# Another order of work in the first stage of a fused encoder block on one Trainium2 core

## The chip, the core and the metric

The kernel runs on one core of a Trainium2 chip. The metric is the device time of one execution in microseconds (us); lower is better. Engines are named as in the profile: PE (TensorE, the matrix products), DVE (VectorE), ACT (ScalarE), POOL (GpSimd) and SP (SyncE, which issues nearly all DMAs here).

## What is computed

One layer of a post-norm block on 256 tokens of width 1024, all in float32. Cut to what matters here:

```python
mod = silu(c) @ w_ada + b_ada                  # (1, 6144)
sh1, sc1, g1, sh2, sc2, g2 = split(mod, 6)
u = normalize(x) * (1 + sc1) + sh1             # (256, 1024)
proj = u @ w_in                                # q, k, v of 8 heads, a forget gate, gated linear attention, merge gates
x = post_norm(alpha * x + (1 + g1) * mixer(proj), ln1_g, ln1_b)
u = normalize(x) * (1 + sc2) + sh2
x = post_norm(alpha * x + (1 + g2) * moe(u), ln2_g, ln2_b)   # top 4 of 32 experts
```

The mixer is a forgetting attention of 8 heads, a gated linear attention of 4 heads, their two output projections, a gated merge and one more projection. The experts read 403 MB of weights, most of all that is loaded.

## The kernel before, in words

The program has three parts. The **first stage** (lines 587 to 849) makes u and the q, k and v of the attention. The **dense blocks** multiply u and what follows from it by the rest of w_in, the branch weights and w_out; side tasks (attention, gates, scans) are put between their products by a planner, `Tasks` with `Pace`, which keeps an estimated clock for each engine and lets a task take its next step when that clock says that its inputs are there. The **expert stage** streams the weights of 32 experts. All loads go through `Ring`, which issues the next load on SP's queue as soon as a buffer is free, in the fixed order in which the loads were asked for. A list of 12 buffers is open to it in the first stage, so that its loads run several rounds ahead.

Everything in the first stage is written out by hand, in program order, and each engine works through its instructions in that order. For accuracy a dense operand is split in two: `split` (line 674) has ACT write the high part in the fast float32 format (fp32r) and DVE or POOL the difference to the original; `three` (line 451) then issues three products, high by high, high by low, low by high.

The stage runs over k = 0 to 7, 128 input features each. What belongs to a k:

- `ada_sum(k)` (line 762): 16 products of 32 x 256 of `csrep`, the silu of c laid out over 32 columns, with a block of w_ada of 1 MB (two DMAs). They leave four partial sums of shift and scale in the PSUM bank `pa`.
- `ada_cols(k)` (line 773): DVE copies the sums to SBUF (`mod`, in the buffer LQ); two products of one column each ("the columns" below) add the four parts up and turn them to a column in the bank `pb`; DVE adds the bias (`shc`); ACT writes the high part of u (`uh`, buffer U1), DVE u itself in place (`nT`, buffers GS and GX) and then the low part (`ul`, buffer U2).
- `row_parts(k)` (line 785): ACT, DVE and POOL split the rows of w_in for q and k (1024 columns, the low part in two halves, one on DVE and one on POOL) and for v (512 columns, low part on POOL), into two of the buffers W0, W1, AD, AM.
- 24 products of 256 columns for q and k, 6 products of 512 columns for v.
- two steps of `masks()` (line 640), a generator that builds the mask constants on DVE: 13 instructions up to the first `yield`, then 3 for each of six levels.

Ahead of them x is normalised (lines 617 to 628) and transposed by PE, in four groups of four transposes, `x_T(hf, tb)` (line 750): `hf` is the half of the features, `tb` the half of the tokens. PE's order in the loop of before is (lines 809 to 829):

```python
sums[k + 1] = ada_sum(k + 1)
for cb in range(8): three(...)            # q and k products of k
ahead[k + 1] = row_parts(k + 1)
ada_cols(k + 1, sums.pop(k + 1))
for tb in range(2): three(pv[tb], ...)    # v products of k
next(ms, None); next(ms, None)            # two steps of the masks
```

After k = 7's q and k products stand 24 products of 32 columns for the forget and low-rank gates (`ff_mm`, line 731), and the dense blocks follow.

All engine calls go through a wrapper, so that the profile gives line 209 for every instruction; they are told apart by tiles. A tile's name in the profile is that of its buffer: a pair such as W0 and W1 stands as W, U1 and U2 as U1U, GS and GX as GSGX; `b` is a PSUM bank.

Of the kernel before, what the change touches and what calls it, by code (L numbers as in the profile page):

```python
# [377 lines left out]
def block_kernel(ctx, tc, x, c, w_ada, b_ada, w_in, fox_f_bias, w_gla_gate, b_gla_gate, gla_norm_g,  # L378
# [236 lines left out]
        ACT.activation(mv[:, 2:3], mv[:, 3:4], AF.Exp, scale=-0.5)  # L615

    nT = gst.now([128, 4, T]), gst.now([128, 4, T])
    for tb in range(2):
        st = bn_tile()
        for i in range(2):  # L620
            DVE.bn_stats(st[:, i, :], xn[tb][:, i * 512:(i + 1) * 512])
        mv = mean_var(st)
        rstd(mv)
        if tb:
            DVE.tensor_scalar(xn[tb], xn[tb], mv[:, 0:1], mv[:, 2:3], op0=OP.subtract, op1=OP.mult)
        else:
            DVE.scalar_tensor_tensor(mv[:, 3:4], mv[:, 0:1], -1.0, mv[:, 2:3], op0=OP.mult, op1=OP.mult)
            ACT.activation(xn[tb], xn[tb], AF.Identity, bias=mv[:, 3:4], scale=mv[:, 2:3])


    strict = small("strict", [128, 128], BF16)
# [8 lines left out]
    def masks():  # L640
        trio = consts.now([128, 128])
        DVE.tensor_scalar(trio, jp, 0.0, None, op0=OP.is_ge)
        DVE.tensor_scalar(strict, jp, 0.0, None, op0=OP.is_gt)
        DVE.tensor_scalar(after, jp, 0.0, NEG, op0=OP.is_gt, op1=OP.mult)
        DVE.tensor_copy(identb, ident)
        DVE.memset(onesb, 1.0)
        DVE.tensor_copy(trior[:, 0:128], trio)
        DVE.tensor_copy(trior[:, 128:256], ones)
        xr = consts.now([128, 128], I32)
        DVE.tensor_tensor(xr, pi, ji, op=OP.bitwise_xor)  # L650
        xrf = consts.now([128, 128])
        DVE.tensor_copy(xrf, xr)
        DVE.tensor_scalar(tri64, xrf, 64.0, 1.0 / 16.0, op0=OP.is_lt, op1=OP.mult)
        DVE.tensor_tensor(tri64, tri64, trio, op=OP.mult)
        upm = consts.now([128, 128])
        DVE.scalar_tensor_tensor(upm, jp, 0.0, xrf, op0=OP.is_gt, op1=OP.mult)
        a = consts.now([128, 64])
        yield
        for L in LEVELS:
            yield  # L660
            m = lvl[L] = small(f"lv{L}", [128, 64])
            u3 = upm.rearrange("p (n two l) -> p n two l", two=2, l=L)[:, :, 1, :]
            DVE.tensor_scalar(m.rearrange("p (n l) -> p n l", l=L), u3, float(L), None, op0=OP.is_ge)
            DVE.tensor_scalar(a.rearrange("p (n l) -> p n l", l=L), u3, float(2 * L), None, op0=OP.is_lt)
            DVE.tensor_tensor(m, m, a, op=OP.mult)
# [96 lines left out]
    def ada_sum(c):  # L762

        w = ring[first["a", c]].rearrange("p k a n -> p k (a n)")
        s = pa[:, c % 2 * 256:c % 2 * 256 + 256]
        for k in range(KC):
            j = k % 4
            PE.matmul(s[32 * j:32 * j + 32, :], csrep[:, k, :], w[:, k, :],
                      start=(k < 4), stop=(k >= 4), skip_group_check=True)
        done(first["a", c])  # L770
        return s

    def ada_cols(c, s):
        mod = la.now([128, 256])
        DVE.tensor_copy(mod, s)
        for i in range(2):
            PE.matmul(pb[:, 2 * c + i:2 * c + i + 1], mod[:, i * 128:(i + 1) * 128], stack[:, 0:1], start=True, stop=True)
        la.put(mod)
        DVE.tensor_tensor(shc[:, :, c], pb[:, 2 * c:2 * c + 2], cols[:, 16 + c:32:8], op=OP.add)
        u = nT[c // 4][:, c % 4, :]  # L780
        ACT.activation(uh[:, c, :], u, AF.Identity, bias=shc[:, 0, c:c + 1], scale=shc[:, 1, c:c + 1])
        DVE.tensor_scalar(u, u, shc[:, 1, c:c + 1], shc[:, 0, c:c + 1], op0=OP.mult, op1=OP.add)
        DVE.tensor_tensor(ul[:, c, :], u, uh[:, c, :], op=OP.subtract)

    def row_parts(k):
        w = ring[first["w", k]]
        qk = split(w[:, 0:2, :].rearrange(FLAT), DVE if k else POOL, POOL)
        v = split(w[:, 2, :], POOL)
        done(first["w", k])
        return qk, v  # L790

    def back():
        for n in ("AD", "AM"):
            if reg[n] in pair.free:
                pair.free.remove(reg[n])

    LA = 2
    ms = masks()
    for tb in range(2):
        x_T(0, tb)  # L800
    pa, pb = aux.now(), aux.now()
    sums = {0: ada_sum(0)}
    ahead = {0: row_parts(0)}
    ada_cols(0, sums.pop(0))
    for tb in range(2):
        x_T(1, tb)
    gle.put(*xn)
    pqk, pv = [mm.now() for _ in range(4)], [aux.now(), aux.now()]
    for k in range(KC):
        qk, v = ahead.pop(k)  # L810
        if k + 1 < KC:
            sums[k + 1] = ada_sum(k + 1)
        for cb in range(8):
            cs = slice(cb * 128, (cb + 1) * 128)
            three(pqk[cb // 2][:, (cb % 2) * T:(cb % 2 + 1) * T], (qk[0][:, cs], qk[1][:, cs]), u_of(k),
                  k == 0 and cb % 2 == 0, k == KC - 1)
        pair.put(qk[2])
        if k + 1 < KC:
            ahead[k + 1] = row_parts(k + 1)
            ada_cols(k + 1, sums.pop(k + 1))  # L820
        if k == KC - 1:
            back()
            for q in range(LA):
# [1292 lines left out]
```

## Time and profile before

| | |
|---|---|
| median of 3 runs | 1268.77 us (1267.07 to 1268.92) |
| the profiled execution | 1269.44 us, span 1267.6 us |
| mean granted TensorE clock | 0.988 |
| PE busy | 1170.3 us, 92% of the span |
| DVE, ACT, POOL busy | 494.6, 265.5, 73.2 us |
| loaded | 471.57 MB, 372 GB/s over the span |

Times in the rows further down are us from the start of the span. A row of the timeline gives start, duration, engine, line, operation, out<-in, shapes and the number of instructions merged into it; in brackets the idle time of the engine just before it and what ended that. SPq is SP's queue of DMA issues. Busy times overlap across engines, and PE's ends are modelled, so starts say more than ends.

### The profile page before, as it was taken

The page shows a single profiled execution, that of the slowest core. Times are in us where ns is not written, and L with a number is a line of the kernel's source. Part 1 is how long each engine was busy: PE and PEld are TensorE (multiplying, and loading weights), DVE is VectorE, ACT ScalarE, POOL GpSimd, SP SyncE. Part 2 cuts the span into 40 slices and gives each one's busy share as a digit, 9 for nine tenths or more (in the row PEclk, how much of TensorE's full clock was granted, in tenths as well). Part 3 has the DMA queues.
Part 4 walks back from the last instruction along what each step waited for, and adds up shares of the span by engine and source line. Part 5 has one row for each costly group of instructions (what it writes and reads, how often), then busy time and mean ns, then how long its engine had stood idle before and what let it go on. Part 6 is the DMA issues. An engine that isn't in the chain of part 4 may idle for free. (4 is left out here: it accounts for less than half of the span.)

```text
span 1267.6 us, 15762 instructions
## 1 busy us (share of the span) xinstructions
PE 1170.3 (92%) x6482; PEld 601.1 (47%) x6482; DVE 494.6 (39%) x1070; ACT 265.5 (21%) x525; POOL 73.2 (6%) x53
## 2 busy tenths in 40 slices
PE   6999999999699999999989989898989898889995
PEld 4797777898434434344333424242433333343432
DVE  5646754477433232324322232222233232222333
ACT  3355445443311111011010101010101101010101
POOL 3412322010000000000000000000000000000000
PEclk9999999999799899999999999999999999999998
DMA  9954347995999999999999999999999999999994
GB/s 306 317 160 133 133 164 263 392 355 226 373 400 429 413 427 428 428 426 428 428 428 429 426 427 429 425 429 428 427 426 429 429 425 428 428 428 428 427 413 143
DMA packets 74118, 471.57 MB, mean 372 GB/s; under 512 B 8637, under 2 KB 29149, under 8 KB 47034
## 3 DMA queue, kind: packets, MB, share of 16 engines
q1 hardware_dynamic: 73850, 470.23, 91.2%
q8 instruction: 53, 0.87, 0.3%
q10 hardware_dynamic: 192, 0.27, 0.1%
q14 instruction: 23, 0.19, 0.0%
HBM read 469.44 MB, written 1.05 MB: 371 GB/s over the span
## 5 line engine op out<-in xcount | busy, mean ns | idle before, releaser
L209 PE MATMUL b<-U1U,W 128*128 128x256 f32 (+1 forms) x840 | 143.1, 410 | 10.8 <-DMA U1U<-in_w_down_dram 8.3
L209 DVE COPY W<-b 128x512 f32<-128x512 f32 x32 | 22.1, 692 | 291.7 <-PE b L209 291.7
L209 PEld LDWEIGHTS b<-U1U,W 128*128 128x128 f32 (+1 forms) x840 | 86.8, 170 | 69.6 <-issue 60.4
L209 DVE TENSOR_TENSOR W<-b,SP 128x512 f32<-128x512 f32 (+1 forms) x33 | 22.3, 676 | 221.3 <-PE b L209 221.3
L209 DVE TENSOR_TENSOR GL<-b,GL 128x512 f32<-128x512 f32 x124 | 77.0, 684 | 54.0 <-PE b L209 54.0
L209 PE MATMUL b<-YB1NB,W 128*64 128x512 f32 (+2 forms) x440 | 89.4, 528 | 5.7 <-DVE SP L209 4.0
L209 PE MATMUL b<-YAW,W 128*64 128x512 f32 (+1 forms) x384 | 82.3, 555 | 6.5 <-DVE SP L209 5.3
L209 PE MATMUL b<-R2YB,W 128*64 128x512 f32 x344 | 78.2, 595 | 8.9 <-DMA R2YB<-in_w_down_dram 7.1
L209 PE MATMUL b<-GSGX,W 128*64 128x512 f32 x336 | 76.2, 595 | 10.3 <-DMA GSGX<-in_w_down_dram 8.5
L209 PE MATMUL b<-R0R,W 128*64 128x512 f32 (+1 forms) x368 | 80.2, 578 | 4.1 <-DMA R0R<-in_w_up_dram 3.7
L209 PE MATMUL b<-LQFA,W 128*64 128x512 f32 x336 | 78.5, 610 | 3.9 <-DMA LQFA<-in_w_up_dram 3.9
L209 ACT ACTIVATE W<-b 128x512 f32<-128x512 f32 x32 | 19.1, 597 | 298.7 <-PE b L209 298.7
L209 PE MATMUL b<-GVKB,W 128*64 128x512 f32 x336 | 76.4, 597 | 5.0 <-DMA GVKB<-in_w_up_dram 5.0
L209 PE MATMUL b<-ADAM,W 128*64 128x512 f32 x336 | 75.9, 593 | 4.0 <-DVE SP L209 4.0
L209 ACT ACTIVATE SP<-b 128x256 f32<-128x256 f32 (+1 forms) x34 | 12.8, 377 | 308.7 <-PE b L209 308.7
L209 PEld LDWEIGHTS b<-W,QA 128*128 128x128 f32 x512 | 63.6, 202 | 15.1 <-DVE GL L209 11.4
L209 PE MATMUL b<-W,QA 128*128 128x128 f32 x512 | 66.7, 291 | 0.5 <-DVE rk L209 0.5
L209 PE MATMUL b<-W,SP 64*128 64x512 f32 (+1 forms) x264 | 63.9, 602 | 0.5 <-DVE W L209 0.5
L209 PEld LDWEIGHTS b<-YB1NB,W 128*64 128x64 f32 (+1 forms) x440 | 35.7, 146 | 56.4 <-issue 45.0
L209 ACT ACTIVATE W<-b,scol 128x128 f32<-128x128 f32 x124 | 46.8, 456 | 65.7 <-PE b L209 60.0
L209 POOL TENSOR_TENSOR GL<-GL,QB 128x512 f32<-128x512 f32 x2 | 2.9, 1426 | 954.1 <-ACT GL L209 954.0
L209 PEld LDWEIGHTS b<-YAW,W 128*64 128x64 f32 (+1 forms) x384 | 30.7, 144 | 55.0 <-issue 43.3
(339 smaller groups left out, 1383.5 us busy)
## 6 DMA issues: line engine op xcount, KB each, us to landing
GVKB<-in_w_up_dram SPq DMA_DIRECT2D x21, 2048.0 KB
R0R<-in_w_up_dram SPq DMA_DIRECT2D x20, 2048.0 KB
LQFA<-in_w_up_dram SPq DMA_DIRECT2D x20, 2048.0 KB
YB1NB<-in_w_up_dram SPq DMA_DIRECT2D x11, 2048.0 KB
U1U<-in_w_up_dram SPq DMA_DIRECT2D x11, 2048.0 KB
YAW<-in_w_up_dram SPq DMA_DIRECT2D x11, 2048.0 KB
GSGX<-in_w_up_dram SPq DMA_DIRECT2D x11, 2048.0 KB
YAW<-in_w_down_dram SPq DMA_DIRECT2D x10, 2048.0 KB
```

The lines of the kernel that those rows point to most:

```text
L209: r = f(*a, **k)
```

## The change

- x: both halves of the tokens are normalised by DVE; before, ACT did the first.
- `ada_sum(0)` comes ahead of all transposes. Of the transposes, x_T(1, 0) comes behind the columns of k = 0, x_T(1, 1) and `ada_sum(1)` between the two halves of the q and k products of k = 0.
- The copy of the sums to SBUF belongs to `ada_sum` now, right behind its products.
- In each round the columns and all of `ada_cols(k + 1)`, then the split of the weights of k + 1, stand between the first and the second half of the q and k products of k (for k = 0 behind both). In the loop of before the split stood ahead of `ada_cols`.
- For k = 0 the split is written out: the first half of the low part goes to DVE instead of POOL, behind the low part of u.
- `masks()` gets more `yield`s: two or three DVE instructions for a step.

```diff
     nT = gst.now([128, 4, T]), gst.now([128, 4, T])
+    mvs = []
     for tb in range(2):
         st = bn_tile()
         for i in range(2):
             DVE.bn_stats(st[:, i, :], xn[tb][:, i * 512:(i + 1) * 512])
-        mv = mean_var(st)
-        rstd(mv)
-        if tb:
-            DVE.tensor_scalar(xn[tb], xn[tb], mv[:, 0:1], mv[:, 2:3], op0=OP.subtract, op1=OP.mult)
-        else:
-            DVE.scalar_tensor_tensor(mv[:, 3:4], mv[:, 0:1], -1.0, mv[:, 2:3], op0=OP.mult, op1=OP.mult)
-            ACT.activation(xn[tb], xn[tb], AF.Identity, bias=mv[:, 3:4], scale=mv[:, 2:3])
+        mvs.append(mean_var(st))
+        rstd(mvs[tb])
+    for tb, mv in enumerate(mvs):
+        DVE.tensor_scalar(xn[tb], xn[tb], mv[:, 0:1], mv[:, 2:3], op0=OP.subtract, op1=OP.mult)
...
         DVE.tensor_scalar(strict, jp, 0.0, None, op0=OP.is_gt)
+        yield
         DVE.tensor_scalar(after, jp, 0.0, NEG, op0=OP.is_gt, op1=OP.mult)
         DVE.tensor_copy(identb, ident)
+        yield
         DVE.memset(onesb, 1.0)
         DVE.tensor_copy(trior[:, 0:128], trio)
         DVE.tensor_copy(trior[:, 128:256], ones)
+        yield
         xr = consts.now([128, 128], I32)
         DVE.tensor_tensor(xr, pi, ji, op=OP.bitwise_xor)
         xrf = consts.now([128, 128])
         DVE.tensor_copy(xrf, xr)
+        yield
         DVE.tensor_scalar(tri64, xrf, 64.0, 1.0 / 16.0, op0=OP.is_lt, op1=OP.mult)
         DVE.tensor_tensor(tri64, tri64, trio, op=OP.mult)
+        yield
         upm = consts.now([128, 128])
         DVE.scalar_tensor_tensor(upm, jp, 0.0, xrf, op0=OP.is_gt, op1=OP.mult)
         a = consts.now([128, 64])
-        yield
         for L in LEVELS:
             yield
...
         done(first["a", c])
-        return s
-
-    def ada_cols(c, s):
         mod = la.now([128, 256])
         DVE.tensor_copy(mod, s)
+        return mod
+
+    def ada_cols(c, mod):
...
-    def row_parts(k):
-        w = ring[first["w", k]]
-        qk = split(w[:, 0:2, :].rearrange(FLAT), DVE if k else POOL, POOL)
-        v = split(w[:, 2, :], POOL)
+    def qk_parts(k):
+        return split(ring[first["w", k]][:, 0:2, :].rearrange(FLAT), DVE, POOL)
+
+    def v_parts(k):
+        v = split(ring[first["w", k]][:, 2, :], POOL)
         done(first["w", k])
-        return qk, v
+        return v
...
+    def qk_mm(k, qk, cbs):
+        for cb in cbs:
             cs = slice(cb * 128, (cb + 1) * 128)
             three(pqk[cb // 2][:, (cb % 2) * T:(cb % 2 + 1) * T], (qk[0][:, cs], qk[1][:, cs]), u_of(k),
                   k == 0 and cb % 2 == 0, k == KC - 1)
...
-    for tb in range(2):
-        x_T(0, tb)
     pa, pb = aux.now(), aux.now()
-    sums = {0: ada_sum(0)}
-    ahead = {0: row_parts(0)}
-    ada_cols(0, sums.pop(0))
+    mods = {0: ada_sum(0)}
     for tb in range(2):
-        x_T(1, tb)
-    gle.put(*xn)
-    pqk, pv = [mm.now() for _ in range(4)], [aux.now(), aux.now()]
+        x_T(0, tb)
+    ahead = {}
+    part_0 = ring[first["w", 0]][:, 0:2, :].rearrange(FLAT)
+    t0 = pair.now()
+    wh0, wl0 = t0[:, 0:1024].bitcast(F32R), t0[:, 1024:2048].bitcast(F32R)
+    ACT.activation(wh0, part_0, AF.Copy)
+    POOL.tensor_tensor(wl0[:, 512:1024], part_0[:, 512:1024], wh0[:, 512:1024], op=OP.subtract)
+    ada_cols(0, mods.pop(0))
+    DVE.tensor_tensor(wl0[:, 0:512], part_0[:, 0:512], wh0[:, 0:512], op=OP.subtract)
+    ahead[0] = (wh0, wl0, t0), v_parts(0)
+    x_T(1, 0)
+    pqk = [mm.now() for _ in range(4)]
     for k in range(KC):
         qk, v = ahead.pop(k)
-        if k + 1 < KC:
-            sums[k + 1] = ada_sum(k + 1)
-        for cb in range(8):
-            cs = slice(cb * 128, (cb + 1) * 128)
-            three(pqk[cb // 2][:, (cb % 2) * T:(cb % 2 + 1) * T], (qk[0][:, cs], qk[1][:, cs]), u_of(k),
-                  k == 0 and cb % 2 == 0, k == KC - 1)
+        if 0 < k < KC - 1:
+            mods[k + 1] = ada_sum(k + 1)
+        qk_mm(k, qk, range(4))
+        if k == 0:
+            mods[1] = ada_sum(1)
+            x_T(1, 1)
+            gle.put(*xn)
+            pv = [aux.now(), aux.now()]
+            qk_mm(k, qk, range(4, 8))
+        if k + 1 < KC:
+            ada_cols(k + 1, mods.pop(k + 1))
+            ahead[k + 1] = qk_parts(k + 1), v_parts(k + 1)
+        if k:
+            qk_mm(k, qk, range(4, 8))
         pair.put(qk[2])
-        if k + 1 < KC:
-            ahead[k + 1] = row_parts(k + 1)
-            ada_cols(k + 1, sums.pop(k + 1))
```

PE at the start of the stage, from behind the transposition of the small vectors to the first columns of k = 1. Products of `ident` are transposes of x (buffer GL), 32x256 are the sums of w_ada, 128x1 the columns, 128x256 the q and k products (a row is one bank, 6 products). Before:

```order
L209 MATMUL b_68<-ident,GL 128x128 x4
L209 MATMUL b_69<-ident,GL 128x128 x4
L209 MATMUL b_70<-YB1NB,LQFA 32x256 x8
L209 MATMUL b_67<-stack,LQFA 128x1 x2
L209 MATMUL b_68<-ident,GL 128x128 x4
L209 MATMUL b_69<-ident,GL 128x128 x4
L209 MATMUL b_70<-QB,LQFA 32x256 x8
L209 MATMUL b_63<-U1U_71,W_72 128x256 x6
L209 MATMUL b_64<-U1U_71,W_72 128x256 x6
L209 MATMUL b_65<-U1U_71,W_72 128x256 x6
L209 MATMUL b_66<-U1U_71,W_72 128x256 x6
L209 MATMUL b_67<-stack,LQFA 128x1 x2
```

The same stretch of PE in the changed kernel:

```order
L209 MATMUL b_68<-YB1NB,LQFA 32x256 x8
L209 MATMUL b_70<-ident,GL 128x128 x4
L209 MATMUL b_67<-ident,GL 128x128 x4
L209 MATMUL b_69<-stack,LQFA 128x1 x2
L209 MATMUL b_70<-ident,GL 128x128 x4
L209 MATMUL b_63<-U1U_71,W_72 128x256 x6
L209 MATMUL b_64<-U1U_71,W_72 128x256 x6
L209 MATMUL b_68<-QB,LQFA 32x256 x8
L209 MATMUL b_67<-ident,GL 128x128 x4
L209 MATMUL b_65<-U1U_71,W_72 128x256 x6
L209 MATMUL b_66<-U1U_71,W_72 128x256 x6
L209 MATMUL b_69<-stack,LQFA 128x1 x2
```

The sums of k = 0 moved ahead of the transposes; the sums of k = 1 and the last four transposes, which stood ahead of all q and k products, now stand amid them.

DVE in one round with two level steps of the masks (`lv`, YAW). The copy of the sums is `COPY LQFA<-b`; then come `shc`, u (GSGX), the low part of u (U1U), and the low part of the weights, a `TENSOR_TENSOR` of 128x512. Before:

```order
L209 TENSOR_TENSOR W_72<-GVKB,W_72 128x512
L209 COPY LQFA<-b_70 128x256
L209 TENSOR_TENSOR shc<-b_67,cols 128x2
L209 TENSOR_SCALAR GSGX<-GSGX,shc 128x256
L209 TENSOR_TENSOR U1U_71<-GSGX,U1U_71 128x256
L209 TENSOR_SCALAR lv_329<-YAW_74 128x64
L209 TENSOR_SCALAR YAW_74<-YAW_74 128x64
L209 TENSOR_TENSOR lv_329<-lv_329,YAW_74 128x64
```

In the changed kernel:

```order
L209 COPY LQFA<-b_68 128x256
L209 TENSOR_TENSOR shc<-b_69,cols 128x2
L209 TENSOR_SCALAR GSGX<-GSGX,shc 128x256
L209 TENSOR_TENSOR U1U_71<-GSGX,U1U_71 128x256
L209 TENSOR_TENSOR W_72<-R0R_107,W_72 128x512
L209 TENSOR_SCALAR lv_430<-YAW_74 128x64
L209 TENSOR_SCALAR YAW_74<-YAW_74 128x64
L209 TENSOR_TENSOR lv_430<-lv_430,YAW_74 128x64
```

The low part of the weights moved from ahead of the copy, behind the masks, to a place ahead of the masks, right behind the low part of u.

In the dense blocks the planner, whose estimated clocks start from other values, puts side tasks at other places, and some loads go to other buffers; the loads ahead of the expert stage are the same ones.

## Rows read from the trace of the kernel before

**Rows 1.** Stretches: us, length, busy (x) of five engines, PEclk, DMA share, GB/s.

```profile
0.00:9.00 9.00, 0.28 (x1) 0.18 (x1) 4.51 (x15) 2.77 (x5) 1.00 (x8) 1.00 0.81 243
...
310.00:320.00 10.00, 9.29 (x60) 7.46 (x58) 4.58 (x11) 4.22 (x9) 0.00 (x0) 1.00 0.34 116
...
400.00:1240.00 840.00, 780.77 (x3800) 314.19 (x3798) 261.75 (x621) 96.23 (x234) 0.00 (x0) 1.00 1.01 426
```

**Rows 2.** Waits of PE, 66 to 318 us: total us, times, longest.

```profile
PE b L209 <- DVE QA L209: 0.3, 1, 0.3
PE b L209 <- DVE SP L209: 0.2, 1, 0.2
```

**Rows 3.** Timeline of PE in the rounds: start, us, operation [idle before].

```profile
29.99 0.61 PE L209 MATMUL b<-stack,LQFA 128*128 128x1 f32 x4 [1.53 <-DVE LQFA L209]
...
45.84 3.14 PE L209 MATMUL b<-U1U,W 128*128 128x256 f32 x24
...
52.24 3.14 PE L209 MATMUL b<-U1U,ADAM 128*128 128x256 f32 x24
...
58.16 3.13 PE L209 MATMUL b<-U1U,W 128*128 128x256 f32 x24
61.12 0.50 PE L209 MATMUL b<-stack,LQFA 128*128 128x1 f32 x4
...
63.43 3.02 PE L209 MATMUL b<-U1U,ADAM 128*128 128x256 f32 x23 [0.19 <-DVE U1U L209]
66.28 0.97 PE L209 MATMUL b<-U1U,YAW 128*32 128x256 f32 x7
```

**Rows 4.** Timeline of PE in the head of the stage.

```profile
12.24 1.93 PE L209 MATMUL b<-YB1NB,LQFA 128*32 128x256 f32 x16
14.72 1.01 PE L209 MATMUL b<-stack,LQFA 128*128 128x1 f32 x4 [0.55 <-DVE LQFA L209]
15.59 1.95 PE L209 MATMUL b<-ident,GL 128*128 128x128 f32 x8
17.47 1.94 PE L209 MATMUL b<-QB,LQFA 128*32 128x256 f32 x16
19.33 3.23 PE L209 MATMUL b<-U1U,W 128*128 128x256 f32 x24
22.40 0.50 PE L209 MATMUL b<-stack,LQFA 128*128 128x1 f32 x4
...
24.33 1.07 PE L209 MATMUL b<-LQFA 128*32 128x256 f32 x16
```

**Rows 5.** Timeline of ACT and DVE in the head of the stage.

```profile
12.02 1.58 ACT L209 ACTIVATE W<-QA 128x1024 fp32r<-128x1024 f32 x2 [0.66 <-DMA QA<-in_w_in_dram]
...
17.11 0.42 DVE L209 TENSOR_TENSOR U1U<-GSGX,U1U 128x256 fp32r<-128x256 f32 x1
```

**Rows 6.** Timeline of DVE and POOL in two rounds, with and without mask steps.

```profile
45.27 2.54 POOL L209 TENSOR_TENSOR ADAM<-R2YB,ADAM 128x512 fp32r<-128x512 f32 x2 [3.88 <-ACT ADAM L209]
45.39 1.24 DVE L209 TENSOR_TENSOR lv<-lv,YAW 128x64 f32<-128x64 f32 x1
...
46.56 1.30 DVE L209 TENSOR_SCALAR lv<-YAW 128x64 f32<-128x64 f32 x1
...
47.78 0.18 DVE L209 TENSOR_SCALAR YAW<-YAW 128x64 f32<-128x64 f32 x1
48.00 0.23 DVE L209 TENSOR_TENSOR lv<-lv,YAW 128x64 f32<-128x64 f32 x1
...
48.74 0.42 DVE L209 COPY LQFA<-b 128x256 f32<-128x256 f32 x1
...
51.14 0.42 DVE L209 TENSOR_TENSOR U1U<-GSGX,U1U 128x256 fp32r<-128x256 f32 x1
...
51.64 0.69 DVE L209 TENSOR_TENSOR W<-QA,W 128x512 fp32r<-128x512 f32 x1
51.68 3.04 POOL L209 TENSOR_TENSOR W<-QA,W 128x512 fp32r<-128x512 f32 x2 [3.87 <-ACT W L209]
```

More of the change, by code (lines that the diff above doesn't have):

```diff
@@ L795, in back @@
                 pair.free.remove(reg[n])
-    LA = 2
-    ms = masks()
-    for tb in range(2):
-        x_T(0, tb)
-    pa, pb = aux.now(), aux.now()
-    sums = {0: ada_sum(0)}
-    ahead = {0: row_parts(0)}
-    ada_cols(0, sums.pop(0))
-    for tb in range(2):
-        x_T(1, tb)
-    gle.put(*xn)
-    pqk, pv = [mm.now() for _ in range(4)], [aux.now(), aux.now()]
-    for k in range(KC):
-        qk, v = ahead.pop(k)
-        if k + 1 < KC:
-            sums[k + 1] = ada_sum(k + 1)
-        for cb in range(8):
+    def qk_mm(k, qk, cbs):
+        for cb in cbs:
             cs = slice(cb * 128, (cb + 1) * 128)
@@ L816, in block_kernel @@
                   k == 0 and cb % 2 == 0, k == KC - 1)
+    LA = 2
+    ms = masks()
+    pa, pb = aux.now(), aux.now()
+    mods = {0: ada_sum(0)}
+    for tb in range(2):
+        x_T(0, tb)
[10 more added lines that the diff above has]
+    pqk = [mm.now() for _ in range(4)]
+    for k in range(KC):
+        qk, v = ahead.pop(k)
+        if 0 < k < KC - 1:
[12 more added lines that the diff above has]
+            qk_mm(k, qk, range(4, 8))
         pair.put(qk[2])
-        if k + 1 < KC:
-            ahead[k + 1] = row_parts(k + 1)
-            ada_cols(k + 1, sums.pop(k + 1))
         if k == KC - 1:
```

## The prediction

> **What bounds the kernel now.** I read the stretches of the program first, then PE's waits, then PE's own order of time in the first stage, and last the other engines inside one round of that stage.
>
> From the expert stage on the transfers are the limit: 426 GB/s over 840 us at a DMA share of 1.01, and a mean granted clock of 1.00 [rows 1]. Just ahead of it the queue starves: 116 GB/s between 310 and 320 us, because the buffers that the expert weights go to are still held by the dense products [rows 1]. So the expert stage starts when the dense products end, and what the first stage gains or loses reaches the end unchanged, if the dense blocks between keep their length. They are pure PE work: between 66 and 318 us PE waits for others twice, 0.5 us in all [rows 2]. A reader should see that nothing there can give time back, and that a wait that the change puts into the first stage is not absorbed later.
>
> The first stage is PE's too, with waits. A round k is: sums of w_ada for k+1 (16 products, 1.07), q and k products (24), two columns of modulation, V products. Without mask steps on DVE a round takes 58.16 - 52.24 = 5.92 us; with them 52.24 - 45.84 = 6.40, and the one behind the long first chunk of masks has PE waiting 1.53 us for DVE ahead of the columns at 29.99 [rows 3]. That waits for the copy of the sums to SBUF, which stands on DVE behind the masks.
>
> **The change, part by part.** All durations are of the one profiled execution, 1269.44 us with a span of 1267.6; the median of the runs is 0.67 lower.
>
> *Nothing:* x's first half is normalised by DVE instead of ACT (the work is ready before PE wants it, since PE now does a 1.93 us group first); the bytes, their order and SP's queue in this stage are unchanged.
>
> *Head, up to the columns of k=1* (before: 22.40 [rows 4]). The first w_ada block is in after x: 1.05 + 1.05 MB at the 243 GB/s of the first 9 us make 8.6 [rows 1]; the next, w_in's 0.79 MB, was waited for until 12.02 [rows 5], which at the same rate points back to 8.8. I take 9.0. Then, at the rates of the old head: 16 products 1.93 and eight transposes 1.95 [rows 4] give 12.9 for the columns of k=0. From there to the low half of u took 17.11 + 0.42 - 14.72 = 2.81 [rows 4, 5], so 15.7. The low part of the q and k weights now follows it on DVE: 0.69 if POOL lets it, 16.5 [rows 6]; but POOL's part for V, 2.54 / 2 = 1.27, is due at the same moment and then holds DVE, 17.4. I take 17.2, since the V part is ready first. From 17.2 PE has to do 12 products, the sums of k=1, 4 transposes and 12 products more, all of which but the q and k products lay ahead of 19.33 before. In the fast rows that is 2.96 (61.12 - 58.16) [rows 3] + 1.07 + 0.55 = 4.6, in the slow ones 1.93 / 1.07 = 1.8 times that, 8.2. So the columns of k=1 come at 21.7 to 25.4, that is -0.7 to +3.0.
>
> Which? The windows print a granted clock of 1.00 from the start [rows 1], but the same 16 products took 1.93 and 1.94 at 12.24 and 17.47 and 1.07 from 24.33 [rows 4]: the array was at 1.2 GHz until about 19.3, when it had worked without a gap since 15.59, and at 2.4 after. With the change there is a gap of some 2 us just ahead of 17.2. Nearest to that is the stretch from 14.72 to 19.33, slow to its end; a part of the 4.6 will be slow and the rest fast. I take the middle: 23.5, **+1.1 us**. The Trainium skill (TensorE: Matmul & The Clock Gate, section What's actually happening) says that the throttled state is the default and that sustained activity releases it; by that rule alone, which speaks against a gap ahead of the products, the head would cost the +3.0 of the slow rows rather than +1.1. Its direction agrees with the 1.93 and 1.07 of this trace.
>
> *Six rounds, from the columns of k=1 to those of k=7* (before: 61.12 - 22.40 = 38.72 [rows 3, 4]). The columns now stand amid the q and k products, where PE has slack, but DVE's loop is what counts, and its order is now: copy of the sums, shift and scale, u, low half of u, low part of the next weights, masks, next copy. From the copy to the end of the low half of u: 51.14 + 0.42 - 48.74 = 2.82. Then DVE and POOL start on the weights together; POOL's two parts end at 51.68 + 3.04 = 54.72, 3.16 later [rows 6]. A mask step that finds POOL at work takes until POOL's part is over: 1.24 and 1.30 us instead of 0.23 and 0.18 [rows 6]. Before, two or three mask steps were through before POOL began and the weights' part came last; now every mask step comes behind it, so the first waits for POOL's first part and the second for its second. A round is then 2.82 + 3.16 + 0.05 = 6.03 plus the remaining steps, 0.37 for two (47.86 to 48.23) [rows 6] less 0.09 of overlap: 6.31 for the four steps of k=0 and for the five of k=1 (the memset doesn't wait), 6.13 for the three of k=2, 6.68 for the six of k=3, 4 and 5. Sum 38.8: **0.0**. The small steps take the 1.53 off one round; the place behind the weights gives it back in all six, each 0.2 to 0.8 over PE's 5.92.
>
> *Tail.* From the last columns to the first forget-gate product (66.28 - 61.12 = 5.16 [rows 3]) PE now also has the second half of the q and k products of k=6, 2.96 / 2 = 1.48; the wait of 0.19 for u at 63.43 goes. 1.3, or 1.1 if more of the pause at 63.43 goes with it: **+1.2**. (This is the other side of moving the columns ahead of them.)
>
> *Dense blocks.* The planner's clock starts from other values, so dozens of side-task rows of PE change places in these blocks, and buffers of loads rotate; the work and the bytes ahead of the expert stage are the same. Where PE waited 0.5 us [rows 2] there is nothing to gain; a new wait could be as long as the 1.53 at 29.99 [rows 3]. I take **+0.3**, ends 0 and 1.5.
>
> Sum: 1.1 + 0.0 + 1.2 + 0.3 = +2.6 us: 1272.0 for a profiled execution like this one, 1271.4 against the median.
>
> **The rivals.**
> *Fast array (0.18).* POOL lets DVE's weights through or the clock is up by 17.2: the head costs -0.7 to 0. Sum +0.5 to +1.5, 1269.3 to 1270.3. For it: PE works from 9.0 on nearly without a pause until about 15. Against: so it did from 14.72 to 19.33 before, at 1.2 GHz [rows 4].
> *The waits vanish (0.10), the other side.* If the mask steps slip past POOL, the copy of the sums is over before PE reaches the columns and all six rounds go at PE's 5.92: 35.5 instead of 38.8, -3.3. With the head as forecast -0.7, 1268.1; with the fast head -2.5, 1266.2. It decides where DVE's masks end less than 3.1 us behind the low half of u, against 3.2 to 3.9 above. Against: both rows of 1.24 and 1.30 [rows 6].
> *Late clock or a new wait (0.12).* The head all slow, +3.0, or a dense block that waits as PE did at 29.99: +4 to +6, 1272.8 to 1274.8.
> *Forecast (0.60).* +1.5 to +4.0.
>
> **How the numbers follow.** 0.2% is 2.5 us, about what a measurement of this kernel tells from no change. Forecast: six tenths of it lie above that, 0.36, and with the third rival 0.12 makes 0.48 slower. The rest of the forecast, the first rival and half of the second: 0.46 the same. Faster is the second rival with the fast head: 0.06. The range leaves out the ends of the second and third rivals: -0.8 to +4.8, 1268.0 to 1273.6.
>
> **What would show it.** Right: the columns of k=1 at 23 to 24 us; the 16 products of k=1 still at 1.9; in each of the first six rounds PE waiting 0.2 to 0.8 for DVE's copy, and mask steps of about 1.2 behind POOL; the forget-gate products at 68 to 69 instead of 66.28; PE's waits between there and 320 still under 1 us; the expert loads starting later by the same amount. Wrong: rounds of 5.9 (the lock does not bite), columns of k=1 ahead of 22 (the clock), or a first stage that is later with an end that is not, which would mean that the expert stage does not start from the dense products' end.

## The result, and the profile after

The changed kernel takes 1278.72 us (median of 4, 1276.41 to 1281.75) against 1268.66 beside it: ratio 1.0087, 95% interval 1.0075 to 1.0099, so it is slower, by 10.1 us between the medians. The forecast was 1271.4 with a range up to 1273.6. The side was right, the size was not: four times what was forecast. The profiled execution is the slowest of the four, 1281.75 us with a span of 1280.0.

Where its 12.4 us of span went is read from five marks: the columns of k=1 and of k=7, the first gate product, the first expert load that waits for the dense products (GVKB from w_up), and the end. The kernels of the experiments are in the same table; each is told of below.

| profile of | columns k=1 | columns k=7 | gates | GVKB load | span | gates to GVKB |
|---|---|---|---|---|---|---|
| before | 22.40 | 61.12 | 66.28 | 318.74 | 1267.6 | 252.46 |
| after | 24.25 | 63.60 | 69.85 | 330.50 | 1280.0 | 260.65 |
| after, again (e8) | 25.00 | 63.56 | 69.81 | 326.10 | 1274.6 | 256.29 |
| e1 after, order of before | 24.68 | 63.05 | 69.29 | 321.73 | 1270.7 | 252.44 |
| e2 before, order of after | 20.82 | 59.52 | 64.68 | 320.96 | 1268.9 | 256.28 |
| e3 before, small masks | 20.35 | 56.34 | 61.60 | 314.06 | 1262.1 | 252.46 |
| e4 and masks in the pause | 22.58 | 57.98 | 63.14 | 315.59 | 1264.0 | 252.45 |
| e5 e1, masks in the pause | 24.01 | 57.97 | 64.11 | 319.12 | 1267.9 | 255.01 |
| e6 e1, second half behind | 23.51 | 62.35 | 68.59 | 322.38 | 1271.7 | 253.79 |
| e7 after, one step to DVE | 25.11 | 63.48 | 69.72 | 325.97 | 1274.7 | 256.25 |
| e9 after, exponential later | 24.53 | 63.07 | 69.31 | 325.87 | 1273.4 | 256.56 |
| e11 e9, four steps off POOL | 23.87 | 63.39 | 69.62 | 322.71 | 1273.8 | 253.09 |
| e10 e5 with 8 transposes | 22.67 | 56.63 | 62.77 | 316.46 | 1265.3 | 253.69 |
| e13 e5 with 24 | 22.96 | 56.92 | 63.06 | 318.08 | 1265.5 | 255.02 |
| e14 e10 again | 22.75 | 56.71 | 62.85 | 315.28 | 1263.6 | 252.43 |
| e12 e4 with a warm head | 20.34 | 57.20 | 62.36 | 317.42 | 1265.7 | 255.06 |

So 3.6 us are lost up to the gates, 8.2 in the dense blocks (gates to GVKB), 0.6 behind. From the GVKB load to the end all these profiles take 947.4 to 949.5 us, but for e11 with 951.1: the expert stage passes on what it is given.

The first stage after, from PE's timeline (columns as in [rows 3]):

```profile
15.49 0.58 PE L209 MATMUL b<-U1U,W 128*128 128x256 f32 x1
17.63 3.11 PE L209 MATMUL b<-U1U,W 128*128 128x256 f32 x11 [1.56 <-DVE U1U L209]
20.67 1.72 PE L209 MATMUL b<-QB,LQFA 128*32 128x256 f32 x16
...
24.25 0.50 PE L209 MATMUL b<-stack,LQFA 128*128 128x1 f32 x4
...
30.39 0.61 PE L209 MATMUL b<-stack,LQFA 128*128 128x1 f32 x4 [1.52 <-DVE LQFA L209]
...
57.09 0.61 PE L209 MATMUL b<-stack,LQFA 128*128 128x1 f32 x4 [0.35 <-DVE LQFA L209]
...
63.60 0.61 PE L209 MATMUL b<-stack,LQFA 128*128 128x1 f32 x4 [0.35 <-DVE LQFA L209]
...
69.85 2.33 PE L209 MATMUL b<-U1U,YAW 128*32 128x256 f32 x19
```

These answer to [rows 3, 4]. The columns of k=1 are 1.85 later than at 22.40, a round with level masks takes 63.60 - 57.09 = 6.51, and from the last columns to the gates it is 6.25 instead of 5.16. One round of DVE and POOL shows why 6.51, against [rows 6]:

```profile
46.52 3.09 POOL L209 TENSOR_TENSOR W<-R0R,W 128x512 fp32r<-128x512 f32 x2 [3.21 <-ACT W L209]
47.08 1.27 DVE L209 TENSOR_SCALAR lv<-YAW 128x64 f32<-128x64 f32 x1
...
48.49 1.20 DVE L209 TENSOR_TENSOR lv<-lv,YAW 128x64 f32<-128x64 f32 x1
...
50.10 0.42 DVE L209 COPY LQFA<-b 128x256 f32<-128x256 f32 x1
```

Both of POOL's parts hold one mask step each, and the copy of the sums comes behind them, as forecast.

What was not forecast stands in the dense blocks: a new wait, and a clock that falls. PE's waits from 66 to 320 us, and then stretches (columns as in [rows 1]):

```profile
PE b L209 <- ACT GVKB L209: 2.8, 1, 2.8
PE b L209 <- DVE QA L209: 0.3, 1, 0.3
```

```profile
32.20:35.70 3.50, 3.50 (x17) 2.23 (x20) 3.40 (x6) 1.10 (x2) 2.84 (x2) 0.51 1.08 331
...
66.00:104.00 38.00, 37.67 (x285) 33.81 (x284) 20.09 (x30) 19.76 (x30) 8.88 (x5) 1.00 0.48 151
104.00:110.80 6.80, 6.80 (x31) 5.32 (x31) 2.32 (x10) 4.23 (x18) 0.00 (x0) 0.50 0.49 154
...
131.40:134.70 3.30, 0.79 (x5) 0.36 (x4) 3.30 (x7) 2.69 (x4) 1.56 (x1) 1.00 0.67 276
134.70:141.50 6.80, 6.47 (x27) 2.98 (x31) 6.76 (x10) 3.05 (x12) 6.80 (x5) 0.50 0.01 4
```

PEclk is about 0.50 in three stretches up to 320 us, half of 2.4 GHz; the profile of before has none between its clock's rise at 19.5 and there. The first begins behind the wait of 1.52 ahead of 30.39, the third at 134.68, at the end of the wait of 2.8 (which lasts to 135.03). The second begins, with no wait, within a group of narrow products (8 rows deep, 64 rows, bf16) that starts at 100.98; the same two products take 0.61 us there and 1.00 behind the fall (timeline of PE):

```profile
100.98 0.61 PE L209 MATMUL b<-YB1NB 8*128 8x384 f32 x2
...
104.20 1.00 PE L209 MATMUL b<-YB1NB 8*128 8x384 f32 x2
```

PE is busy 6.80 of 6.80 us there: a share of busy time does not show that it runs at half speed, only the clock column does.

### The profile page after: what moved, and what is told of

Same layout as the page of the kernel before. It is cut to its first block, busy times and chain, and to the rows that moved or that the text cites. A ratio compares the mean times of both kernels' runs of the same rounds, so it can differ in the third digit from the quotient of the medians.

```text
span 1280.0 us, 15767 instructions
## 1 busy us (share of the span) xinstructions
PE 1180.1 (92%) x6482; PEld 607.3 (47%) x6482; DVE 508.6 (40%) x1070; ACT 265.3 (21%) x524; POOL 81.0 (6%) x53
## 5 line engine op out<-in xcount | busy, mean ns | idle before, releaser
L209 PE MATMUL b<-U1U,W 128*128 128x256 f32 (+1 forms) x840 | 147.8, 415 | 12.4 <-DMA U1U<-in_w_down_dram 8.3
L209 PEld LDWEIGHTS b<-U1U,W 128*128 128x128 f32 (+1 forms) x840 | 90.0, 174 | 72.2 <-issue 59.9
L209 PE MATMUL b<-GSGX,W 128*64 128x512 f32 x336 | 77.9, 606 | 11.8 <-DMA GSGX<-in_w_down_dram 8.4
```

The lines of the kernel that those rows point to most:

```text
L209: r = f(*a, **k)
```

## Experiments

Where a kernel is said to have the order of the dense blocks of before (or after), the planner's clocks are set at the end of the first stage, ahead of `back()` at k = 7, to those that it has there in that kernel; from the gates on every engine's instructions then stand in that order, row for row.

```diff
+STATE = ({'PE': 70.9094, 'DVE': 68.3123, 'ACT': 65.2333, 'POOL': 67.0456, 'DMA': 76.1891},
...
         if k == KC - 1:
+            pace.set(STATE, [aux.free[0], aux.free[1], *pv])
             back()
```

### e1 and e2: first stage and dense order apart

> First stage of the changed kernel; at its end the planner's clocks are set to those that it had there in the kernel before, so that from the forget-gate products on every engine's order is row for row that of before. Theory A (the re-planned order of the dense blocks costs the most: the new wait of 2.91 us at 131.97 and two stretches at half clock, 103.96 and 134.68): only the first stage's +3.6 is left, or +2.2 if the half clock at 32.28 stays away too: 1270.9 to 1272.3, no wait over 0.6 us and no half clock between 70 and 320. Theory B (the order doesn't matter; the array slows because the same groups of small products come 3.6 us later): half clock stays between 95 and 140, 1274 to 1279.

> The other way round: first stage of before, and from the forget-gate products on the changed kernel's order, row for row. Theory A: the wait for ACT near 128 and the half clock come here too: +6 to +9 on before, 1275 to 1278, with the forget-gate products at 66.3 as before. Theory B: +0 to +1, 1268.7 to 1270; the wait may be there, but no half clock.

Measured: e1 1273.34 us, ratio 1.0043 (1.0026 to 1.0060); e2 1274.95 us, 1.0057 (1.0040 to 1.0073). Each alone makes the kernel slower, and together they come near the change's 1.0087. The dense blocks take 252.44 us in e1, as before, and in e2 256.28, as in e8; the profile of e2 has the wait again (its waits of PE from 66 to 320, then the stretch around it):

```profile
PE b L229 <- ACT GVKB L229: 2.8, 1, 2.8
```

```profile
126.80:131.10 4.30, 4.20 (x19) 2.37 (x23) 4.26 (x5) 2.34 (x11) 4.30 (x3) 0.60 0.00 0
```

So the order of the dense blocks brings the wait, with the old first stage as well; theory A holds for the wait. (For the half clock inside the narrow products it does not, see e8.) e1's end is later than expected (1270.9 to 1272.3): its first stage costs more than one profile of before had shown, for which the head below gives at least part of the reason. e2's profile alone would mislead: its span is only 1.3 us over that of before, because its columns of k=1 happened to come 1.6 us earlier.

### e8: the same kernel again

> The changed kernel once more, every engine's order as it was: which of the stretches at half clock come again. If the order of the work alone sets them: again from about 32, 104 and 135. If it only makes them possible: the wait of 2.8 near 132 and the waits of the first stage come again to 0.2 us, the stretches at half clock come elsewhere or are missing, and the span moves with them between 1274 and 1280.

One execution, 1276.47 us. The wait is 2.82 again, and the half clock behind it is there again, but half as long; the one inside the narrow products at 101 is not. The first stage has one from 17.0 to 23.8 instead of the one at 32:

```profile
17.00:23.80 6.80, 6.21 (x33) 4.42 (x34) 1.72 (x4) 0.00 (x0) 0.23 (x1) 0.50 1.13 328
...
131.90:136.40 4.50, 4.39 (x19) 2.19 (x23) 4.46 (x6) 2.55 (x11) 4.50 (x4) 0.62 0.00 0
```

So with every engine's order and the waits the same, two executions of this kernel differ in where the clock falls. All sixteen profiles hold the group of narrow products between 91 and 107 us. In seven (after, e5, e6, e9, e10, e12, e13) the clock halves inside it, in the others, that of before among them, it doesn't. These are five of the ten profiles with the dense order of before and two of the six with the changed one, so nothing here says that the change brings it; what does stays open. A half clock there costs 1.2 to 3.0 us of an execution; where it stays away, and no wait is there, gates to GVKB is 252.43 to 252.46. Behind a wait of 2.8 the half clock came in after, e2 and e8, but not behind the one of 2.87 in e9. The profile of after is 4.4 us longer there than e8: 3.0 in that group (from 100.98 to the next block's first product at 110.94, in e8 from 100.93 to 107.93), and 1.4 behind the wait.

### e7, e9 and e11: where the wait of 2.8 comes from

In the changed order ACT has its evictions of PSUM behind an exponential that waits for DVE (timeline of ACT, after):

```profile
129.63 0.60 ACT L209 ACTIVATE GVKB<-b 128x512 f32<-128x512 f32 x1 [1.67 <-PE b L209]
132.01 1.06 ACT L209 ACTIVATE GL<-GL 128x1024 f32<-128x1024 f32 x1 [1.78 <-DVE GL L209]
...
133.92 1.06 ACT L209 ACTIVATE GVKB<-b 128x512 f32<-128x512 f32 x2
```

e7 gives one of POOL's products to DVE (the 18th choice of `either`), the planner's clocks left as they were:

```diff
-        (DVE if d + bias <= q else POOL).tensor_tensor(o, a, b, op=op)
+        e = DVE if d + bias <= q else POOL
+        calls.append(e.name)
+        if len(calls) - 1 == SWAP:
+            DVE.eng.tensor_tensor(o, a, b, op=op)
+            pace.book("POOL", "tensor_tensor", (o, a, b), [])
+        else:
+            e.tensor_tensor(o, a, b, op=op)
```

> The changed kernel with its own dense order; one elementwise product of the GLA block (128x1024, GSGX from QB and GL, on POOL at 126.15 for 2.39 us) runs on DVE at the same place of the order, the planner's clocks going on as if it were on POOL. Theory: POOL's product holds DVE (the split of the weights took 2.56 instead of 1.23, the two GL steps 2.38 instead of 1.36), so ACT's exponential waits 1.78 for GL, the evictions behind it on ACT come late and PE waits 2.84 at 131.97. Then PE's wait there falls to 0 to 1.6 and the half clock behind it is shorter or gone: 1273 to 1276. Rival (the order on ACT alone makes the wait): 2.3 to 2.9 remain, 1278.

It missed: 1276.64 us, 1.0073 (1.0056 to 1.0090). The wait fell to 1.1 at its place, but another came ahead of it, 2.5 in all:

```profile
PE b L209 <- DVE GSGX L454: 1.4, 1, 1.4
PE b L209 <- ACT GVKB L209: 1.1, 1, 1.1
```

e9 moves one instruction on ACT alone: the exponential's issue is held back until three instructions behind it are issued. These are the next split and two evictions of PSUM, where the expectation speaks of three evictions.

```diff
+                if self.count == LATE[0]:
+                    self.held = (f, a, k)
+                    self.pace.book(self.name, op, a, [])
+                    return None
             r = f(*a, **k)
+            if self.name == "ACT" and op == "activation" and self.count == LATE[1]:
+                g, ga, gk = self.held
+                g(*ga, **gk)
```

> The changed kernel with its own dense order; on ACT alone one instruction changes its place: the exponential of GL at 132.01 (which waited 1.78 for DVE) stands behind the three evictions of PSUM that followed the next split. Theory, since moving one product from POOL to DVE (e7) only moved the wait: ACT's order makes it, an eviction whose bank PE needs stands behind an instruction that waits for DVE. Then PE's wait of 2.8 near 132 falls to 0.2 to 0.8 and the half clock behind it is gone: from the forget-gate products to the first expert load 253 to 254 us instead of 256.3; 1273 to 1275. Rival (the banks would be late in any order, since DVE and POOL are behind as a whole): a wait of the same length some us later, 1276 to 1278.

A miss as well: the wait is the rival's, and the time lies between the two, 1275.16 us, 1.0065 (1.0037 to 1.0092). The wait leaves its place and comes again, as long, ten us later (timeline of PE, then of DVE and POOL, in e9):

```profile
130.41 0.61 PE L215 MATMUL b<-YB1NB 8*128 8x384 f32 x2 [0.22 <-ACT GVKB L215]
...
140.43 1.87 PE L215 MATMUL b<-LQFA,GSGX 128*64 128x64 f32 x32 [2.87 <-DVE ADAM L215]
```

```profile
132.02 2.31 DVE L215 TENSOR_TENSOR YAW<-R0R,YAW 128x1024 fp32r<-128x1024 f32 x1
133.21 6.33 POOL L215 TENSOR_TENSOR GL<-GVKB 128x512 f32<-128x512 f32 x4
...
134.85 1.56 DVE L215 TENSOR_TENSOR GSGX<-QB,GL 128x1024 f32<-128x1024 f32 x1
...
136.54 2.09 DVE L215 TENSOR_SCALAR SP<-SP,sm 128x128 f32<-128x128 f32 x2
```

DVE is late as a whole, and its instructions are long while POOL runs (1.21 and 0.48 without it, in e11 below). e11 takes POOL's four GL differences away (choices 25, 26, 28 and 29 to DVE, as in e7), on top of e9.

> e9 (the exponential behind the evictions; its wait of 2.87 for DVE stood at 140.43) with four more instructions moved: the GL differences of two levels (128x512, from 133.21 on POOL, 6.33 us in all) run on DVE, at the place of the order where they were issued, which is behind the sum into ADAM that PE waits for. Theory: it is POOL's products that make DVE late there (the split took 2.31 instead of 1.21, a product 1.56 instead of 1.21, two scalings 2.09 instead of 0.48, 3.1 us in all), so with POOL idle DVE comes to ADAM some 3 us earlier, and PE's wait falls from 2.87 to 0 to 0.7, without another in its place: 252.5 to 254 from the forget-gate products to the first expert load if no half clock falls into it (1.3 to 3.4 more if one does), 1272 to 1274. Rival (DVE has too much to do there in any case): the wait comes again some us later, 256 and 1275.

The same instructions of DVE in e11, and PE's wait:

```profile
133.66 1.21 DVE L215 TENSOR_TENSOR GSGX<-QB,GL 128x1024 f32<-128x1024 f32 x1
...
134.99 0.48 DVE L215 TENSOR_SCALAR SP<-SP,sm 128x128 f32<-128x128 f32 x2
```

```profile
137.28 1.87 PE L215 MATMUL b<-LQFA,GSGX 128*64 128x64 f32 x32 [0.91 <-DVE ADAM L215]
```

With less on POOL (the four stand on DVE behind this stretch) DVE is through sooner: 1.56 became 1.21 and 2.09 became 0.48, the wait fell to 0.91 and no other came. Gates to GVKB is 253.09, against 252.44 in e1 and 256.56 in e9, whose profile also has a half clock at 104.5. The same piece of work (from DVE's copy of SP to its sum into ADAM) in before, in after and in e11, DVE's busy time third, POOL's fifth:

```profile
115.80:131.87 16.07, 16.07 (x96) 9.72 (x97) 14.60 (x24) 11.69 (x27) 4.91 (x4) 1.00 0.28 99
```

```profile
121.25:142.44 21.19, 18.35 (x93) 10.31 (x94) 18.87 (x23) 11.50 (x29) 16.74 (x9) 0.84 0.17 55
```

```profile
118.05:136.45 18.40, 18.10 (x126) 11.26 (x126) 16.83 (x23) 10.66 (x24) 10.22 (x5) 1.00 0.37 123
```

In the changed order DVE has one instruction fewer there and needs 4.3 us more, while POOL is given 16.74 us of work instead of 4.91. The same instructions got longer, two of them in before, then in after:

```profile
118.47 1.23 DVE L209 TENSOR_TENSOR W<-R0R,W 128x1024 fp32r<-128x1024 f32 x1
...
129.35 0.48 DVE L209 TENSOR_SCALAR SP<-SP,sm 128x128 f32<-128x128 f32 x2
```

```profile
127.05 2.56 DVE L209 TENSOR_TENSOR W<-R0R,W 128x1024 fp32r<-128x1024 f32 x1 [1.19 <-ACT W L209]
...
138.54 2.09 DVE L209 TENSOR_SCALAR SP<-SP,sm 128x128 f32<-128x128 f32 x2
```

POOL was at work throughout both rows of after, and idle during both of before. The Trainium skill (SBUF — State Buffer, section Who interferes with whom) says that a DVE instruction with two SBUF inputs contends with a GpSimd (POOL) instruction that reads SBUF, and that scalings (`tensor_scalar`) can contend with it too; the later one blocks until the first is through. The 2.56 and 2.09 agree: the scalings took 1.61 more, and one of POOL's four differences takes 6.33 / 4 = 1.58.

The time of e11 is 1274.96 us, 1.0049 (1.0033 to 1.0066): its interval lies below that of the change and takes in e1's 1.0043, which has the same first stage and no dense loss. Against e9 alone the intervals overlap, so that POOL's work makes the wait is shown by the traces, not by the time. Its profile lost 2.2 us against before behind the GVKB load, which no other does; that stays open.

### e3 to e6: the rounds of the first stage

e3 gives before the changed `masks()`; e4 also moves the two steps of a round behind the copy of the sums; e5 does the like in the changed kernel. All have the dense order of before.

```diff
         DVE.tensor_copy(mod, s)
+        for _ in range(2 if c else 0):
+            next(ms, None)
```

That is e4; in e5 one step stands here and one behind `shc`, and in both the two calls at the round's end are gone.

> The kernel before with only the masks in the changed kernel's small steps, still behind the V products; dense order held to that of before. If the long first chunk alone made the wait of 1.53: the round from 22.40 takes 6.0 to 6.2 instead of 7.59, the next two 5.9 to 6.1, the three with level masks 6.4; -1.2 to -1.6 at the forget-gate products and at the end, 1267.1 to 1267.5. If small steps run into POOL's parts as in the changed kernel: rounds 6.2 to 6.5 throughout, 0 to -0.4. A half clock in the dense blocks would hide either: then the end tells nothing, only the forget-gate start does.

> As the run with small masks, but the two steps of a round stand behind DVE's copy of the sums, in the pause in which DVE waits for the columns (2.96 us ahead of 55.77). If the place of the masks on DVE is what lengthens the rounds: all six rounds at PE's 5.92, 35.5 instead of 38.72, -3.2 at the forget-gate products (63.1) and at the end, 1265.4. If POOL's lock stretches the steps beyond the pause: rounds 6.1 to 6.4, -1 to -2.

> Changed first stage, dense order of before (as in e1), and the masks' two steps of a round moved on DVE out of the place behind the low part of the weights: one behind the copy of the sums, one behind shc, where DVE waits 0.70 for PE and 0.67 for ACT. If the masks' place is what makes DVE the longer loop: the rounds go at PE's 5.9 but for the first (which has 12 products fewer on PE ahead of its columns and waits anyway), 36 instead of e1's 38.4: -2.4 on e1 at the forget-gate products. If something else on DVE or POOL sets the round (the weights' parts, the low half of u): 6.1 to 6.5 remain, 0 to -0.5.

Measured: e3 1265.80 us, 0.9988 (0.9975 to 1.0001); e4 1265.85, 0.9983 (0.9972 to 0.9995); e5 1269.53, 1.0011 (1.0002 to 1.0021). In e4 and e5 the rounds take 5.90, but for e5's first with 4.46 (it has 12 products fewer): six rounds in 35.40 and 33.96 us instead of 38.72 and e1's 38.37. So the place of the masks on DVE costs the changed kernel 4.4 us, by the intervals of e1 and e5 about 4; DVE's round in e5:

```profile
50.67 0.42 DVE L229 COPY LQFA<-b 128x256 f32<-128x256 f32 x1 [1.48 <-PE b L229]
51.01 0.61 DVE L229 TENSOR_SCALAR lv<-YAW 128x64 f32<-128x64 f32 x1
51.54 0.18 DVE L229 TENSOR_SCALAR YAW<-YAW 128x64 f32<-128x64 f32 x1
```

The copy now waits 1.48 for PE, where PE waited for it. e3's rounds did better than expected: small steps alone, behind the V products, give rounds of 5.9 to 6.0, but for the last with 6.35; in those from 38.19 to 49.99 DVE was through with the masks before POOL began. So the small steps are a gain in the rounds (35.99 us instead of 38.72), though e3's time, whose interval reaches 1.0001, is not told apart from before; their place behind the weights, in the new loop, takes the gain back.

e6 moves the second half of the q and k products of k=0 behind the columns (in e1's kernel):

> Changed first stage, dense order of before (as in e1), one edit: the second half of the q and k products of k=0 stands behind the columns of k=1, as in all later rounds (PE's order alone changes, by one group). Theory: those 12 products stand ahead of the columns of k=1 for nothing and are missing in the round behind, where PE waits 1.5 ahead of the columns of k=2. Then the columns of k=1 come 1.5 earlier than in e1 and the wait in the round behind falls from 1.5 to 0.3; -1.5 at the forget-gate products. Rival (the columns of k=1 wait for the copy of the sums or for the clock, not for these products): 0 to -0.5.

The columns of k=1 come 1.2 earlier and the wait ahead of those of k=2 falls to 0.35, but DVE's copy of a transpose now stands ahead of `shc` and that round takes 6.43 instead of 6.15: 0.7 is left at the gates. 1272.89 us, 1.0035 (1.0023 to 1.0046), not told apart from e1.

### e10, e13 and e14: the head and the clock

The changed head leaves PE waiting for the low half of u behind the first product (1.56 in after, 1.76 in e5). PE's timeline in e5:

```profile
17.59 0.38 PE L229 MATMUL b<-U1U,W 128*128 128x256 f32 x1 [1.76 <-DVE U1U L229]
...
20.12 1.94 PE L229 MATMUL b<-QB,LQFA 128*32 128x256 f32 x16
```

The granted clock had risen at 15.42 and fell again (stretch of e5):

```profile
18.80:22.20 3.40, 3.40 (x25) 1.91 (x24) 0.07 (x1) 0.00 (x0) 0.00 (x0) 0.50 1.09 356
```

So it went in e1, e6, e7 and e8, from 16.3 to 17.1 on; in after, e9 and e11 it rose only at 21.5 to 22.6. In none of these eight profiles was it up all the way from 17 to 21. e10 and e13 add work that nobody needs to e5:

```diff
+    for _ in range(8):
+        PE.transpose(pqk[3][:, 0:128], ident, ident)
     for k in range(KC):
```

> e5 (changed first stage, masks in DVE's pauses, dense order of before) with eight transposes of the identity on PE just ahead of the first q and k product, into a bank that is overwritten behind: work that nobody needs, in the 1.6 us in which PE waits for the low half of u. Theory: the half clock from 16.3 to 18.8 on in four of five profiles with this head comes from PE's pause; with the pause filled the clock stays up and the columns of k=1 come at 22 to 23 instead of 24.0 to 25.1, -1 to -2 on e5: 1268. Rival (these products don't keep the clock up, or its fall has another cause): 24 to 25 again, 1269.5 or up to 0.5 more.

> e10 with 24 transposes instead of 8. In e10 they ran from 14.98 to 15.77 and PE still waited 1.61 for the low half of u, so the pause was not filled, yet the array stayed at full clock. Theory A (the pause is what lowers the clock): 24 transposes, 2.4 us at full clock, close it; no wait over 0.5 ahead of the second q and k product, no half clock before 66, the columns of k=1 at 22 to 23, 1266 to 1267. Theory B (e10's gain was the luck of its executions, or came from elsewhere): half clock again from 16 to 19 on, columns of k=1 at 24 to 25, 1269.5. Theory C (the transposes run on into the time when u is there, because the array is slow): columns at 23.5 to 25 without a half clock.

> e10 once more, for its head. If eight transposes ahead of the pause are enough: full clock from about 14 to 66 again and the columns of k=1 at 22.5 to 23. If that was luck: half clock from 16 to 19 on and the columns at 24 to 25, as in four of the five profiles with this head and no transposes.

PE in e10, then in e13:

```profile
14.98 1.04 PE L229 MATMUL b<-ident 128*128 128x128 f32 x8
...
17.74 0.38 PE L229 MATMUL b<-U1U,W 128*128 128x256 f32 x1 [1.61 <-DVE U1U L229]
...
19.74 1.07 PE L229 MATMUL b<-QB,LQFA 128*32 128x256 f32 x16
```

```profile
14.91 2.78 PE L229 MATMUL b<-ident 128*128 128x128 f32 x24
...
18.04 0.39 PE L229 MATMUL b<-U1U,W 128*128 128x256 f32 x1 [0.23 <-DVE U1U L229]
...
20.03 1.07 PE L229 MATMUL b<-QB,LQFA 128*32 128x256 f32 x16
```

In e10, e13 and e14 the clock stays at 1.00 from its rise (14.0 to 15.7) to 66, the 16 sums take 1.07 instead of 1.94, and the columns of k=1 come at 22.67, 22.96 and 22.75. e10: 1266.76 us, 0.9984 (0.9974 to 0.9995); e13: 1267.01, 0.9992 (0.9981 to 1.0002); e10's interval lies below e5's, e13's touches it. e14's one execution took 1265.42. Eight are as good as 24, though they left a wait of 1.61 (1.11 in e14): the pause need not be closed, so theory A of e13, that it alone lowers the clock, is not borne out. Products in PE's idle time ahead of it were enough here. Whether a shorter pause would have done it too, and how much work is enough, was not tried.

### e12: the old head, warm

```diff
+    for _ in range(16):
+        PE.transpose(bank[3][:, 0:128], ident, ident)
     for tb in range(2):
         x_T(0, tb)
```

> e4 (the kernel before with small masks in DVE's pause) with sixteen transposes of the identity on PE from about 5.5 on, where PE waits for x until 9.61, into a bank that is overwritten later. If PE's pauses in the head decide when the clock comes up (e10): it is up before 14 in each run, the sums of k=0 and k=1 take 1.0 instead of 1.9, the columns of k=1 come at 19.5 to 20.5 instead of 20.4 to 22.6, -1 to -2.5 on e4, 1264. Rival (this early work doesn't count, the pause behind it undoes it): as e4, 1265.9.

1264.34 us, 0.9973 (0.9963 to 0.9984), 3.4 us under before by the ratio, the lowest of all, but not told apart from e4's 0.9983 (0.9972 to 0.9995). The clock rose at 10.18 and the sums of k=0 and k=1 took 1.07 each. The columns of k=1 came at 20.34 (22.58 in e4), and then two rounds took 6.39 and 6.87: the splits of the weights waited 2.10 and 1.44 for their loads, in e4 not at all. Of the 2.2 us won in the head, 0.8 are left at the gates.

## Why the prediction was wrong

**What bounds the kernel.** Right. The expert stage starts where the dense products end and passes the difference on.

**Head, +1.1.** Measured +1.85 in the profile of after, 1.5 to 2.7 in those of e1, e5, e7, e8, e9 and e11, inside the bounds of -0.7 to +3.0. The second q and k product came at 17.63, against 17.2, but by another way, so that the closeness is in part luck: the first sums started at 10.06, not 9.0, and POOL held DVE in the low half of u itself (1.42 us at 16.16, where before has 0.42), and not in the weights' part behind it (0.68). The 4.6 to 8.2 behind it took 6.6. What the step missed is that before's own 22.40 is a late one: with the old head the columns of k=1 came at 20.35 to 22.58 (e2, e3, e4), by when the clock rose (13.97 to 19.55). Over the four profiles with the old head and the seven with the new one the means are 21.5 and 24.5: the head costs about 2.9, near the end of +3.0 and not the middle. The rule of the Trainium skill (TensorE: Matmul & The Clock Gate, section What's actually happening), that activity releases the throttle, spoke against the pause. e10 and e13, where added products kept the clock up, agree with it.

**Six rounds, 0.0.** Right in mechanism and size: 6.15, 6.43, 6.23 and three times 6.52 in e1 against 6.31, 6.31, 6.13 and 6.68, sum 38.37 against 38.8. In the profile of after a half clock adds 1.1 to the second (7.52). The first round was not seen: with no second half of products to do, PE waits 1.52 there, and in after and e11 the clock fell behind that.

**Tail, +1.2.** Measured +1.09.

**Dense blocks, +0.3, with ends 0 and 1.5.** This is the step that failed. It measured +8.2, or +3.8 in e8 and e2. Of the 8.2, 2.8 are the wait, 3.0 the half clock inside the narrow products, and the 2.4 that are left go with the half clock behind the wait. The prediction saw that the planner puts dozens of instructions elsewhere and took that to be free, since the blocks before had no waits to lose; its upper end came from a wait of the first stage, where POOL never has more than two parts in a row. It looked at PE's order and not at what POOL was given: in the new order DVE is busy 4.3 us longer beside POOL, and PE waits 2.8. Nor was a fall of the clock in the sum. Behind a wait, the head's own argument had shown it to be possible; the one inside the narrow products, which comes with the order of before as well, nothing in the profile of before had shown.

**The rivals.** *Late clock or a new wait* (0.12, +4 to +6) comes nearest. It named the one or the other; both came, a head at about +2.9 and a dense wait of 2.8 instead of 1.53, with falls of the clock besides, and +10.1 lies beyond it. The waits did not vanish, the fast array did not come. Of the signs that the prediction named, two failed at once: PE's waits up to 320 us were 3.1 instead of under 1, and the expert loads came 11.8 later, not by the 3.6 of the forget-gate products.

The sum against the runs: the first stage alone is 1.0043 of before (5 us, e1), where the forecast had +2.3; the order of the dense blocks alone is 1.0057 (7 us, e2), where it had +0.3. Together they measured 1.0087. That the forecast had the right side rests on the head and the tail; 8.2 of the 12.4 us in the profile of after, and about half of the loss by the times, came from a term that it had put near nothing.

## What to carry to other kernels

Where a planner orders later work by an estimated clock, an edit ahead of it is two changes: hold the later order fixed, time each alone, and compare what each engine is given, not only where PE's rows stand. An instruction that waits behind a slow neighbour should be moved only after asking what the neighbour is slow from: here two moves only shifted the wait, and taking work off POOL besides cut it to 0.91 with no other in its place. Small DVE steps belong where DVE waits for others and the steps have room, not between POOL's work and the copy that PE waits for.

## What the runs showed of the hardware

- Needless products made the kernel faster: 8 transposes in the changed head (e10 against e5), with 1.07 instead of 1.94 for the same 16 products behind them. With 24 the interval touches e5's, and with 16 ahead of the old head it overlaps e4's.
- The clock halved inside a group of narrow products in which PE does not wait, in seven of sixteen profiles; gates to GVKB differs by up to 2.6 us between kernels with the same order for that alone (252.44 in e1, 255.01 in e5).
- With POOL at work two DVE scalings of 128x128 took 2.09 instead of 0.48, and giving four instructions from POOL to DVE made DVE finish sooner.
